# One layer of a hybrid diffusion backbone on one core: an opening with other load rows and column places, and gate and decay work spread over the level products

## The chip, the cores and the metric

The kernel runs on one core of a Trainium2 chip. TensorE (PE) multiplies, VectorE (DVE) and ScalarE (ACT) work on elements, GpSimd (POOL) does some elementwise work and issues a few DMAs, and SyncE (SP) issues the weight loads. Each engine runs its own instructions in a fixed order and waits on semaphores. The metric is the device time of one execution in microseconds (us).

## The reference

One layer over 256 latent tokens `x` and 256 context tokens `ctx`, width 2048, in fp32, with five steps:

1. `h = rms_norm(x) * g * (1 + scale) + shift`, the same for `ctx`, where scale and shift are columns of `silu(c) @ w_mod + b_mod` (`silu(c_ctx)` for the context).
2. One projection `h @ w_in` gives q, k, v of a windowed attention, `qb`, `kb`, `vb` of a gated linear attention (GLA) with 4 heads, a low-rank decay for each of its two directions, and merge gates.
3. Windowed attention (16 query heads, 4 key heads, one learned sink logit each, all context keys in the same softmax).
4. GLA in both directions; the scans of the latent tokens start from the end states of the context. In sums of log decays `b`: `o = A v` with `A[t,s] = sum_d q[t,d] k[s,d] exp(b[t,d] - b[s,d])`, plus a term `q exp(b) S`, where `S = sum_s k[s] exp(b_end - b[s]) v[s]` runs over the context.
5. Merge, output projection, gated residual, then a ConvFFN with width 5632.

The kernel keeps fp32 accuracy on PE by splitting each operand into a high and a low part (`hi`, `lo`) and adding three products: hi x hi, lo x hi, hi x lo.

## The kernel before, in words

**Weights.** `wload` loads two rows of weight tiles at a time (`raw`, 128 x 1024 numbers, 512 KB). `wsplit_raw` turns them into `whi` (ACT, L207) and `wlo` (DVE, L208). `proj_T` and `proj_nat` run the products of one weight block, all through `mm` on L83. Loads go through `load` on SP's queue (L104), and in the opening a chain of order-only dependencies keeps them in program order.

**Opening (L519 to about L640).** The two columns of the modulation (scale and shift) are needed before the first product. They are made in groups of 2, 2, 4, 4 and 4 tiles of 128 channels. `mod_both` (L305 on) makes one group of one of the two: it loads `w_mod` in tiles `mraw` of 1 MB, multiplies them with the two conditioning vectors (`pm`, L95), transposes the result on DVE (`mtr`, L324), turns it into columns with one small product (`pcol`, L95), and copies and adds on DVE (L334, L337). For each group there are so the steps `a0`, `a1` (scale: two `mraw`), `ea` (its `pcol`), and `b0`, `b1`, `eb` for shift. `affine_scale` (L488, DVE) multiplies the tokens by the scale column and the norm factor, `affine_shift` (L495 on ACT, L496 on DVE) adds the shift and splits into `h..hi` and `h..lo`. `h0` is the latent tokens, `h1` the context; their second digit is the half of the channels. `idle(n)` puts n small transposes of a constant on PE (tile `warm`, L519). The work of group 1 and 2 is put between the products of the group ahead of it: `mid()` takes so many prepared steps as the next number of a list says.

**Queue of loads at the start.** SP issues in this order: four parts of `xT`, four `mraw` (group 0), four `raw` (blocks QB, QB+512, KB, VB for the first two tiles), four parts of `ctxT`, four `mraw` (group 1), and so on. Beside it, ACT issues the constants `pack` and `crow`, and POOL issues the broadcast of `attn_sink` to 128 partitions (tile `sink`, L894) as its first DMA.

**GLA heads (`gla_A`, L703 on).** A head's piece of work is a generator whose pieces are taken, one at a time, between the products of a value projection that runs on PE meanwhile (`aside`, called from `tick` and `midway`; 16 places in one block). `with_gla` (L859) sets the rate at which pieces are taken, 0.91 pieces for each place. The pieces of a head are: the gates (four small products `pz`, then five ACT operations each, L721 to L725, and an add on DVE and on POOL); a first product `pa` of `qb` and `kb`; eight levels, in each of which ACT and DVE make scaled `q` and `k` (L766 to L775), DVE adds over halves of segments (L777 to L780) and PE multiplies them (`pa`, L95) one level later, after which DVE copies the result under a mask into `at` (L751); and at the end the decayed keys of the context: four scans on DVE (`kf`, `kg`, L800 and L802), three exponentials on ACT, two multiplies with the keys (L808, L809) and the final products `pa<-q,kf`. Each `pa` stands at a fixed place in PE's order: where its `q`, `k` or `kf` is late, all PE work waits.

Of the kernel before, what the change touches and what calls it, by code (L numbers as in the profile page):

```python
# [8 lines left out]
F32 = mybir.dt.float32  # L9
F32R = mybir.dt.float32r  # L10
U8 = mybir.dt.uint8
AF = mybir.ActivationFunctionType
# [4 lines left out]
P = 128  # L17
# [14 lines left out]
def layer_kernel(ctx, tc, A, out):  # L32
# [90 lines left out]
    def load_tokens(s):  # L123
        for i in range(4):
            k = slice((i % 2) * 4, (i % 2) * 4 + 4)
            load(xr[2 * s + i // 2][:, k, :], A["ctxT" if s else "xT"][i // 2, :, k, :])
# [22 lines left out]
    def defer(n, fn):  # L149

        later.append([n, fn])
# [37 lines left out]
    def wload(src):  # L189
        n = src.shape[0] // P  # L190
        raw = wr.tile([P, 2, 512], F32, name="raw", tag="raw")
        load(raw[:, 0:n, :], src.rearrange("(c p) d -> p c d", p=P))
        return raw
# [113 lines left out]
    def mod_both(part, t0, n, dst, put=None):  # L307
# [5 lines left out]
        def step(k0):  # L313
            if k0 == 0:
                a.append(bank(f"pm{part}_{t0}", (P, w), side=True))
            raw = M("mraw", [P, nk, w])
            load(raw, A["w_mod01"][part, t0 + k0 // nk].rearrange("p (c d) -> p c d", c=nk))
            for k in range(nk):
                kt = k0 + k
                q = 32 * (kt % 4)  # L320
                mm_b(a[0][q:q + 32, :], cS[:, kt, :], raw[:, k, :], start=(kt < 4), stop=(kt >= 12))
            if k0 == KT - nk:
                tr = W2("fb", "mtr", [P, n, 4, 32])
                V.transpose(tr.rearrange("p a b c -> p (a b c)"), a[0])  # L324
                a.append(tr)
                if put is not None:
                    put(end)
# [68 lines left out]
    def rms_scale(ss, n, shape):  # L396
# [16 lines left out]
            for (t0, n), put in zip(groups, [None, None] + 3 * [lambda fn: defer(0, fn)])]  # L413
# [5 lines left out]
    def square_sums(s):  # L419
# [3 lines left out]
        for i in range(4):  # L423
            x_ = xr[2 * s + i // 2][:, (i % 2) * 4:(i % 2) * 4 + 4, :]
            q = wr.tile([P, 4, T], F32, name="sq", tag="raw")
            if s + i:
                S.activation(q, x_, AF.Square)
            else:
                V.tensor_tensor(q, x_, x_, op=ALU.mult)
                parts.extend(q[:, k, :] for k in range(4))  # L430
                continue
# [98 lines left out]
    a0()  # L530
    a1()
# [3 lines left out]
    affine_scale(0, *groups[0])  # L535
    b1()
    raws = [wload(w_in[0:2 * P, c:c + 512]) for c in (QB, QB + 512)]
# [7 lines left out]
    raws = [wload(w_in[0:2 * P, c:c + 512]) for c in (KB, VB)]  # L545
# [4 lines left out]
    proj_T(w_in, QB, kts, [h_all(0)], add_to(lambda i: qb0[i], True))  # L550
    proj_T(w_in, QB + 512, kts, [h_all(0)], add_to(lambda i: qb0[2 + i], True))
# [14 lines left out]
    ea()  # L566
    b0()
    b1()
    for s in range(2):
        affine_scale(s, *groups[1])  # L570
# [4 lines left out]
             lambda i, b: S.activation(vb0[:, 2 + i, :], b, AF.Copy))  # L575
    early.extend(wload(w_in[2 * P:4 * P, c:c + 512]) for c in (QB, QB + 512, KB, VB))
# [19 lines left out]
    for gi, (t0, n) in enumerate(groups):  # L596
# [8 lines left out]
        if gi + 1 < len(groups):  # L605
# [3 lines left out]
            if gi == 1:  # L609
                bg_rate[:] = [0.0, 0.0]  # L610
                steps = iter([1, 2, 1, 2, 2, 0])

                def mid():
                    pin[0] = last[0]
                    for _ in range(next(steps)):
                        bg_steps.pop(0)()
                    pin[0] = None
        if t0 == 8:
            more_h(1)
        for s in range(2):  # L620
            if gi > 1:
                affine_scale(s, t0, n)
                affine_shift(s, t0, n)
# [30 lines left out]
    in_order(last_lo[0], V.tensor_scalar(nbg, nbg, -1.0, None, op0=ALU.mult).ins)  # L654
    lmask = cst.tile([P, 7, P], U8, name="lmask")
# [49 lines left out]
    def gla_A(h, kb, qb, res):  # L705
# [7 lines left out]
        for d in range(2):  # L713
            g_ = W2("fc", "gc", [P, 2, T])
            for dt in range(2):
# [11 lines left out]
                G.tensor_tensor(g_[:, dt, :], mn[:, T:2 * T], e[:, T:2 * T], op=ALU.add)  # L727
            gc.append(g_)
            yield
# [27 lines left out]
        for lv in range(8):  # L757
# [22 lines left out]
            V.tensor_tensor(sbL, sbL, sbR[:, :, 0:1].to_broadcast([P, n, m]), op=ALU.add)  # L780
            if lv == 1:
                yield
            if lv:
                products(lv - 1, *prev)
            prev = q2, k2
            yield
# [8 lines left out]
        kf = W2("fa", "kf", [P, 2, T])  # L795
        kg = W2("fa", "kg", [P, 2, T])
        tot = sm.tile([P, 2], F32, name="tot", tag="tot", bufs=2)
        one = ones[:, 0:1].to_broadcast([P, T])
        for dt in range(2):
            V.tensor_tensor_scan(kf[:, dt, :], one, gc[0][:, dt, :], 0.0, op0=ALU.mult, op1=ALU.add)  # L800
            V.memset(kg[:, dt, 0:1], 0.0)
            V.tensor_tensor_scan(kg[:, dt, 1:T], ones[:, 0:1].to_broadcast([P, T - 1]), gc[1][:, dt, 0:T - 1], 0.0,  # L802
                                 op0=ALU.mult, op1=ALU.add)
        V.tensor_scalar(tot, kf[:, :, T - 1], -1.0 / 16, None, op0=ALU.mult)
        for dt in range(2):
            S.activation(kf[:, dt, :], kf[:, dt, :], AF.Exp, scale=1.0 / 16, bias=tot[:, dt:dt + 1])
        S.activation(kg, kg, AF.Exp, scale=-1.0 / 16)
        V.tensor_tensor(kf, kf, kc, op=ALU.mult)  # L808
        V.tensor_tensor(kg, kg, kc, op=ALU.mult)  # L809
# [47 lines left out]
    def with_gla(h, kb, block):  # L857
        res = []
        beside[:] = [gla_A(h, kb, qbt, res), 0.91, 0.0]  # L859
# [33 lines left out]
    sink = cst.tile([P, 16], F32, name="sink")  # L893
    G.dma_start(sink, A["attn_sink"][0].partition_broadcast(P))  # L894
# [423 lines left out]
```

## Time and profile before

| | |
|---|---|
| median of 3 runs | 1982.68 us (1981.75 to 1982.88) |
| profiled execution | 1981.3 us, span 1979.5 us, mean granted clock 0.999 |
| PE busy in the span | 1955.1 us (99%) |
| DVE, ACT, POOL busy | 1399.8, 972.1, 44.2 us |
| DMA | 420.88 MB, mean 213 GB/s over the span |

The span runs from the first instruction to the last of the profiled execution; the execution's own time is 1.8 us longer. A line of the waits says which engine and line waited, for which producer, the sum, the count and the longest. A line of a timeline gives start, duration, engine, line, operation, output and inputs, the count, and in brackets how long the engine had been idle before and what released it; `x16` of `pm` are 8 matrix products, each of which PE records twice. A line of the table of windows gives busy time and counts for each engine in a stretch, then the granted clock of PE (1.00 is full speed), the busy share of the DMA engines and the bytes moved.

### The profile page before, as it was taken

What the parts mean: (1) busy time and instruction counts of PE and PEld (TensorE: products, weight loads), DVE (VectorE), ACT (ScalarE), POOL (GpSimd) and SP (SyncE); (2) the same over time, 40 slices, a digit from 0 to 9 for tenths busy, and PEclk for the clock granted to TensorE, in tenths of its full rate; (3) what the DMA queues carried; (4) which work ended last, traced back from release to release, by engine and by line L of the source; (5) the groups of instructions that cost most, each with busy time, mean ns of one, the idle gap of its engine ahead of it and who ended that gap; (6) DMA issues with size and microseconds to landing.
All of it is one profiled execution on the core that took longest, in us unless ns stands there. A gap on an engine that the chain in (4) does not pass through costs nothing.

```text
span 1979.5 us, 27075 instructions
## 1 busy us (share of the span) xinstructions
PE 1955.1 (99%) x10292; PEld 1636.0 (83%) x10292; DVE 1399.8 (71%) x2150; ACT 972.1 (49%) x1415; POOL 44.2 (2%) x60
## 2 busy tenths in 40 slices
PE   7999999999999999999999999999999999999999
PEld 5679988888887778888888888888888888888887
DVE  5756767876767988777766467989886555677754
ACT  4323555552345666444444445755555334555533
POOL 0010010012000000000000000000000000000000
PEclk9999999999999999999999999999999999999999
DMA  9966222336754456888888677688886566666563
GB/s 379 413 258 185 75 85 78 93 108 205 233 160 118 127 181 213 268 290 292 289 286 265 235 236 262 198 271 285 257 274 228 193 197 188 187 190 189 188 216 109
DMA packets 183666, 420.88 MB, mean 213 GB/s; under 512 B 12544, under 2 KB 12768, under 8 KB 178800
## 3 DMA queue, kind: packets, MB, share of 16 engines
q1 hardware_dynamic: 182000, 413.45, 63.9%
q0 software_dynamic: 1360, 5.54, 1.0%
q8 instruction: 80, 1.31, 0.3%
q14 instruction: 50, 0.41, 0.1%
q10 hardware_dynamic: 176, 0.17, 0.0%
HBM read 416.98 MB, written 2.13 MB: 212 GB/s over the span
## 4 chain that ended last, share of the span: by engine, by line
PE 68%; DVE 0%; ACT 0%; issue 0%; DVEq 0%
PE acc L83 52%; PE accs L83 12%; PE poa L95 1%; PE pS L95 1%; PE ptp L98 1%; PE pto L98 0%; PE ptx L98 0%; DVE wlo L208 0%; ACT s L986 0%; PE ptq L98 0%; DVE s L991 0%; DVE yd L1238 0%; DVE yd L1232 0%; DVE raw L365 0%; ACT whi L207 0%
## 5 line engine op out<-in xcount | busy, mean ns | idle before, releaser
L208 DVE TENSOR_TENSOR wlo<-raw,whi 128x1024 fp32r<-128x1024 f32 x568 | 694.1, 1223 | 439.9 <-ACT whi L207 396.4
L207 ACT ACTIVATE whi<-raw 128x1024 fp32r<-128x1024 f32 x568 | 601.5, 1060 | 765.9 <-PE acc L83 608.9
L83 PE MATMUL accs<-h,whi 128*128 128x512 f32 x704 | 176.3, 392 | 0.0
L83 PE MATMUL acc<-h,whi 128*128 128x512 f32 x640 | 160.4, 392 | 0.0
L83 PEld LDWEIGHTS accs<-h,whi 128*128 128x128 f32 x704 | 126.6, 189 | 22.7
L83 PE MATMUL acc<-whi,h01hi 128*128 128x512 f32 x352 | 139.9, 398 | 0.0
L83 PE MATMUL acc<-whi,h00hi 128*128 128x512 f32 x352 | 138.9, 395 | 0.0
L83 PE MATMUL acc<-whi,h00lo 128*128 128x512 f32 x352 | 138.1, 392 | 0.0
L83 PE MATMUL acc<-whi,h01lo 128*128 128x512 f32 x352 | 137.8, 392 | 0.0
L83 PE MATMUL acc<-whi,ah 128*128 128x512 f32 x352 | 137.0, 389 | 0.0
L83 PE MATMUL acc<-whi,al 128*128 128x512 f32 x352 | 137.0, 389 | 0.0
L83 PEld LDWEIGHTS acc<-h,whi 128*128 128x128 f32 x640 | 115.0, 189 | 20.6
L83 PEld LDWEIGHTS accs<-h,wlo 128*128 128x128 f32 x704 | 96.0, 190 | 6.9
L83 PE MATMUL acc<-wlo,h01hi 128*128 128x512 f32 x352 | 98.7, 396 | 0.0
L83 PE MATMUL accs<-h,wlo 128*128 128x256 f32 x704 | 98.2, 282 | 0.0
L83 PE MATMUL acc<-wlo,h00hi 128*128 128x512 f32 x352 | 97.8, 394 | 0.0
L83 PE MATMUL acc<-wlo,ah 128*128 128x512 f32 x352 | 94.3, 389 | 0.0
L83 PEld LDWEIGHTS acc<-h,wlo 128*128 128x128 f32 x640 | 87.4, 190 | 6.3
L83 PE MATMUL acc<-h,wlo 128*128 128x256 f32 x640 | 89.4, 282 | 0.0
L365 DVE CUSTOM_DVE_ANT_0 raw<-raw,csrow,pack 128x1024 f32<-128x1024 f32 x64 | 81.4, 1281 | 0.0
L83 PEld LDWEIGHTS acc<-whi,ah 128*128 128x128 f32 x352 | 66.1, 188 | 13.7
L83 PEld LDWEIGHTS acc<-whi,al 128*128 128x128 f32 x352 | 66.1, 188 | 13.7
(377 smaller groups left out, 3558.1 us busy)
## 6 DMA issues: line engine op xcount, KB each, us to landing
raw<-in_w_in SPq DMA_DIRECT2D x208, 512.0 KB, 4.2
raw<-in_w_up SPq DMA_DIRECT2D x176, 512.0 KB, 4.1
raw<-in_w_modT SPq DMA_DIRECT2D x128, 512.0 KB, 4.4
raw<-in_w_down SPq DMA_DIRECT2D x88, 512.0 KB, 3.6
mraw<-in_w_mod SPq DMA_DIRECT2D x32, 1024.0 KB, 12.1
raw<-in_w_attn_o SPq DMA_DIRECT2D x32, 512.0 KB, 5.0
raw<-in_w_gla_o SPq DMA_DIRECT2D x32, 512.0 KB, 5.1
raw<-in_w_out SPq DMA_DIRECT2D x32, 512.0 KB, 4.7
```

Source lines behind the costliest of these rows:

```text
L83: r = pe_seq(PE.matmul(*a, **k))
L95: return pe_seq(after(PE.matmul(*a, **k)))
L98: return pe_seq(after(PE.transpose(*a)))
L207: j = S.activation(hi[:, 0:n, :], raw[:, 0:n, :], AF.Copy).ins
L208: i = V.tensor_tensor(lo[:, 0:n, :], raw[:, 0:n, :], hi[:, 0:n, :].bitcast(F32), op=ALU.subtract).ins
L365: i0 = V.tensor_tensor_reduce(out=raws[i], in0=raws[i], in1=row[0], scale=1.0, scalar=d if h else bmod[:, b0:b0 + 1], op0=ALU.mult, op1=AL ...
```

## The change

**Opening loads.** `xT` and `ctxT` come as two loads of 1 MB, with one row of 8 KB for each partition in place of two loads with rows of 4 KB. The first four weight tiles come from a new input `w_first`, packed on the host, with one row of 4 KB for each partition in place of two of 2 KB. The last load of the shift column of groups 0 and 1 is split into two halves of 512 KB. The broadcast of `sink` moves from the first place of POOL's queue to the place behind `cw`, ahead of `lm` and eight gate weights (`wtm`).

SP's order from the first load on (`xr_85` to `xr_88` are the tokens, `mraw` the modulation weights, `raw` the weight tiles):

```order
-L104 DMA xr_85<-in_xT 128x1024 x2
-L104 DMA xr_86<-in_xT 128x1024 x2
-L104 DMA mraw<-in_w_mod 128x2048 x4
-L104 DMA raw<-in_w_in 128x2x512 x4
-L104 DMA xr_87<-in_ctxT 128x1024 x2
-L104 DMA xr_88<-in_ctxT 128x1024 x2
-L104 DMA mraw<-in_w_mod 128x2048 x4
+L1353 UNCONDITIONAL_BRANCH
+L104 DMA xr_85<-in_xT 128x2048
+L104 DMA xr_86<-in_xT 128x2048
+L104 DMA mraw<-in_w_mod 128x2048 x3
+L104 DMA mraw<-in_w_mod 128x1024 x2
+L104 DMA raw<-in_w_first 128x1024 x4
+L104 DMA xr_87<-in_ctxT 128x2048
+L104 DMA xr_88<-in_ctxT 128x2048
+L104 DMA mraw<-in_w_mod 128x2048 x3
+L104 DMA mraw<-in_w_mod 128x1024 x2
```

Each token tile now has one row in place of two, and behind three `mraw` stand two halves.

**Opening order.** Six transposes (`idle(6)`) are added between `a0` and `a1`, and six before `b1`. The first eviction of `qb0` is an ACT copy as before; its instructions are now remembered, and the squares of the context tokens on ACT are tied behind them. In group 1, `b0` and `b1` come ahead of `ea`, so that all products `pm` of the group come ahead of its first `pcol`. In group 2, the scale's `pcol` moves to a later place together with the multiplication of the tokens (`affine_scale`), and all 16 products of the shift column are taken in one place.

PE at the end of the KB block of group 1 (`pm_4_673`, after it `pm_4_693`, is the shift of group 2, `pcol_4_724`/`pcol_4_740` its columns, `pcol_4_676` the scale's columns; `acc<-h..,wlo` are the last 16 products of KB, `acc<-whi,h00hi` the first of VB). Before, behind the last products of KB:

```order
L83 MATMUL acc<-h00hi,wlo 128x256
L83 MATMUL acc<-h10hi,wlo 128x256
L83 MATMUL acc<-h00hi,wlo 128x256
L83 MATMUL acc<-h10hi,wlo 128x256
L95 MATMUL pm_4_673<-mraw,cS 32x512 x8
L95 MATMUL pcol_4_724<-mtr,pack 32x32
L83 MATMUL acc<-whi,h00hi 128x512
```

After, ahead of the last 16 products of KB:

```order
L83 MATMUL acc<-h10lo,whi 128x256
L95 MATMUL pcol_4_676<-mtr,pack 32x32
L95 MATMUL pm_4_693<-mraw,cS 32x512 x16
L83 MATMUL acc<-h00hi,wlo 128x256
L83 MATMUL acc<-h10hi,wlo 128x256
```

Before, 8 of the shift's 16 products stood ahead of KB's last 16 and 8 behind; now all 16 stand ahead of them, with the scale's columns directly before.

**GLA.** Each of the four gate pieces is now a piece of its own (two before), the extra stop at level 1 is gone, and the rate goes from 0.91 to 0.97, which takes 15 pieces over the 16 places in place of 14. The four scans move from the end of the head into levels 2 and 3, `tot` and the exponentials into level 4, the two multiplies with the keys into level 6; each is tied behind the last add of its level. `kf` and `kg` use another pool (`fb` in place of `fa`).

DVE in the third head (`kf<-ones,gc` and `kg<-ones,gc` are the scans; `segs` the adds of a level; `q`, `k` the scaled operands). Before, at the end of the head:

```order
L794 TENSOR_TENSOR q_3652<-q_3652,qb 128x512
L794 TENSOR_TENSOR q_3653<-q_3653,qb 128x512
L62 TENSOR_TENSOR ats<-at,ats 128x256
L800 SCALAR_TENSOR_TENSOR kf<-ones,gc 128x256
L801 MEMSET kg 128x1
L802 SCALAR_TENSOR_TENSOR kg<-ones,gc 128x255
L62 TENSOR_TENSOR ats<-pa,ats 128x256
L800 SCALAR_TENSOR_TENSOR kf<-ones,gc 128x256
L801 MEMSET kg 128x1
L802 SCALAR_TENSOR_TENSOR kg<-ones,gc 128x255
```

After, between two levels:

```order
L835 TENSOR_TENSOR segs<-segs 128x64x4
L806 COPY_PREDICATED at<-lmask,pa 128x256
L767 SCALAR_TENSOR_TENSOR kf<-ones,gc 128x256
L768 MEMSET kg 128x1
L212 TENSOR_TENSOR wlo<-raw,whi 128x1024
L769 SCALAR_TENSOR_TENSOR kg<-ones,gc 128x255
L823 TENSOR_TENSOR q_3487<-q_3487,qb 128x512
L830 TENSOR_TENSOR k_3491<-k_3491,kb_2020 128x512
L832 TENSOR_TENSOR segs<-segs 128x32x8
L833 TENSOR_TENSOR segs<-segs 128x32x8
L834 TENSOR_TENSOR segs<-segs 128x32x8
L835 TENSOR_TENSOR segs<-segs 128x32x8
```

The scans stood behind the last level; now a pair of them stands between the adds of level 2 and the next `q` and `k`, and the other pair one level later.

The diff, cut to what the text speaks of:

```diff
     def load_tokens(s):
-        for i in range(4):
-            k = slice((i % 2) * 4, (i % 2) * 4 + 4)
-            load(xr[2 * s + i // 2][:, k, :], A["ctxT" if s else "xT"][i // 2, :, k, :])
+        for i in range(2):
+            load(xr[2 * s + i], A["ctxT" if s else "xT"][i])
...
+    def first_w(i):
+        raw = wr.tile([P, 2, 512], F32, name="raw", tag="raw")
+        load(raw.rearrange("p k d -> p (k d)"), A["w_first"][i])
...
-            load(raw, A["w_mod01"][part, t0 + k0 // nk].rearrange("p (c d) -> p c d", c=nk))
+            src = A["w_mod01"][part, t0 + k0 // nk].rearrange("p (c d) -> p c d", c=nk)
+            if t0 < 4 and part == 0 and k0:
+                load(raw[:, 0:nk // 2, :], src[:, 0:nk // 2, :])
+                load(raw[:, nk // 2:nk, :], src[:, nk // 2:nk, :])
+            else:
+                load(raw, src)
...
-                S.activation(q, x_, AF.Square)
+                j = S.activation(q, x_, AF.Square).ins
+                if s and i in (0, 2):
+                    in_order(evicted[i + 1], j)
...
     a0()
+    idle(6)
     a1()
     idle(4)
...
-    raws = [wload(w_in[0:2 * P, c:c + 512]) for c in (KB, VB)]
+    raws = [first_w(i) for i in range(2, 4)]
     load_tokens(1)
     i, j = affine_shift(0, *groups[0])
     hold.append(i)
     hold_hi.extend([None, j])
-    proj_T(w_in, QB, kts, [h_all(0)], add_to(lambda i: qb0[i], True))
-    proj_T(w_in, QB + 512, kts, [h_all(0)], add_to(lambda i: qb0[2 + i], True))
+    evicted = []
+    for j in range(2):
+        proj_T(w_in, QB + j * 512, kts, [h_all(0)],
+               lambda i, b, j=j: evicted.append(S.activation(qb0[2 * j + i], b, AF.Copy).ins))
...
-    ea()
     b0()
     b1()
-    for s in range(2):
-        affine_scale(s, *groups[1])
+    ea()
+    affine_scale(0, *groups[1])
...
+    affine_scale(1, *groups[1])
...
-                steps = iter([1, 2, 1, 2, 2, 0])
+                steps = iter([1, 2, 1, 4, 0, 0])
+
+                def next_columns():
+                    if pend:
+                        pend.pop(0)()
+
+                def scale_2():
+                    next_columns()
+                    for s in range(2):
+                        affine_scale(s, *groups[2])
+
+                also = iter([next_columns] * 3 + [scale_2, next_columns, lambda: affine_shift(0, *groups[2])])
 
                 def mid():
                     pin[0] = last[0]
+                    next(also)()
...
-            if gi > 1:
+            if gi > 2:
                 affine_scale(s, t0, n)
+            if gi > 2 or (gi == 2 and s):
...
+    sink = cst.tile([P, 16], F32, name="sink")
+    G.dma_start(sink, A["attn_sink"][0].partition_broadcast(P))
...
+                yield
             gc.append(g_)
-            yield
...
+        def decays(dt, level):
+            one = ones[:, 0:1].to_broadcast([P, T])
+            i = V.tensor_tensor_scan(kf[:, dt, :], one, gc[0][:, dt, :], 0.0, op0=ALU.mult, op1=ALU.add).ins
+            V.memset(kg[:, dt, 0:1], 0.0)
+            j = V.tensor_tensor_scan(kg[:, dt, 1:T], ones[:, 0:1].to_broadcast([P, T - 1]), gc[1][:, dt, 0:T - 1],
+                                     0.0, op0=ALU.mult, op1=ALU.add).ins
+            in_order(level, i, j)
+
+        def decayed(level):
+            tot = sm.tile([P, 2], F32, name="tot", tag="tot", bufs=2)
+            in_order(level, V.tensor_scalar(tot, kf[:, :, T - 1], -1.0 / 16, None, op0=ALU.mult).ins)
+            for dt in range(2):
+                S.activation(kf[:, dt, :], kf[:, dt, :], AF.Exp, scale=1.0 / 16, bias=tot[:, dt:dt + 1])
+            S.activation(kg, kg, AF.Exp, scale=-1.0 / 16)
+
+        def decayed_keys(level):
+            in_order(level, V.tensor_tensor(kf, kf, kc, op=ALU.mult).ins)
+            in_order(level, V.tensor_tensor(kg, kg, kc, op=ALU.mult).ins)
+
+        beside_levels = {2: lambda i: decays(0, i), 3: lambda i: decays(1, i), 4: decayed, 6: decayed_keys}
...
-            V.tensor_tensor(sbL, sbL, sbR[:, :, 0:1].to_broadcast([P, n, m]), op=ALU.add)
-            if lv == 1:
-                yield
+            level = V.tensor_tensor(sbL, sbL, sbR[:, :, 0:1].to_broadcast([P, n, m]), op=ALU.add).ins
             if lv:
                 products(lv - 1, *prev)
             prev = q2, k2
+            if lv in beside_levels:
+                beside_levels[lv](level)
...
-        for dt in range(2):
-            V.tensor_tensor_scan(kf[:, dt, :], one, gc[0][:, dt, :], 0.0, op0=ALU.mult, op1=ALU.add)
-            V.memset(kg[:, dt, 0:1], 0.0)
-            V.tensor_tensor_scan(kg[:, dt, 1:T], ones[:, 0:1].to_broadcast([P, T - 1]), gc[1][:, dt, 0:T - 1], 0.0,
-                                 op0=ALU.mult, op1=ALU.add)
-        V.tensor_scalar(tot, kf[:, :, T - 1], -1.0 / 16, None, op0=ALU.mult)
-        for dt in range(2):
-            S.activation(kf[:, dt, :], kf[:, dt, :], AF.Exp, scale=1.0 / 16, bias=tot[:, dt:dt + 1])
-        S.activation(kg, kg, AF.Exp, scale=-1.0 / 16)
-        V.tensor_tensor(kf, kf, kc, op=ALU.mult)
-        V.tensor_tensor(kg, kg, kc, op=ALU.mult)
...
-        beside[:] = [gla_A(h, kb, qbt, res), 0.91, 0.0]
+        beside[:] = [gla_A(h, kb, qbt, res), 0.97, 0.0]
```

## What the change does to the time: the prediction

> **What bounds the kernel now.** I read the page first, then the waits of PE in the two stretches that the change touches, then the windows and timelines there.
>
> ```profile
> span 1979.5 us, 27075 instructions
> PE 1955.1 (99%) x10292; PEld 1636.0 (83%) x10292; DVE 1399.8 (71%) x2150; ACT 972.1 (49%) x1415; POOL 44.2 (2%) x60
> ```
>
> PE is busy in 99% of the span. No PE work goes away: 12 small transposes are added. So the change can win only waits of PE, and the slow clock. They are few. The waits of PE from 0 to 80 us, and from 200 to 460 us (the four GLA heads):
>
> ```profile
> PE pm L95 <- DMA mraw<-in_w_mod: 3.0, 3, 1.4
> PE pcol L95 <- DVE mtr L324: 2.6, 4, 0.8
> ...
> PE acc L83 <- ACT qb L503: 0.4, 1, 0.4
> ...
> PE pa L95 <- DVE q L768: 3.1, 4, 1.1
> PE pa L95 <- DVE kf L808: 2.5, 3, 1.0
> ```
>
> With 0.4 and 0.7 for `h00hi` and `h10hi` (rows of the opening below) that is 7.1 us in the opening, and 5.6 us in the heads: the whole stake is about 13 us of 1981.3. The windows show what stands behind the opening's waits (busy time of the engines, granted clock, share and GB/s of DMA last):
>
> ```profile
> 5.00:7.00 2.00, 1.96 (x9) 1.96 (x10) 1.30 (x2) 1.90 (x4) 0.00 (x0) 1.00 1.04 158
> 7.00:10.20 3.20, 3.20 (x12) 2.69 (x11) 0.73 (x2) 3.11 (x3) 0.51 (x1) 1.00 1.02 397
> 10.30:20.20 9.90, 6.86 (x66) 3.41 (x64) 5.67 (x17) 1.89 (x3) 0.00 (x0) 1.00 1.00 421
> 20.30:26.70 6.40, 5.85 (x40) 3.67 (x41) 2.99 (x9) 3.36 (x5) 0.00 (x0) 0.75 1.05 396
> 26.80:31.80 5.00, 4.72 (x40) 4.52 (x38) 4.17 (x6) 3.88 (x6) 0.00 (x0) 1.00 1.04 421
> 60.00:112.00 52.00, 50.08 (x381) 37.15 (x380) 35.00 (x73) 11.56 (x16) 0.00 (x0) 1.00 1.01 402
> ```
>
> The DMA engines are full in all these stretches, so a load's landing is set by what was streamed ahead of it, and time saved in the stream stays saved through the opening. From 5 to 7 us they are as full and move only 158 GB/s: that is where `sink` (128 pieces of 64 bytes, landed at 7.9) is in the stream.
>
> **The loads.** `sink` out of the start: 2 us at 158 in place of 397 GB/s are 0.48 MB missing, or 1.2 us. The 2 KB rows of the four `raw` ran at 396 GB/s (20.3 to 26.7), 8 KB rows of `mraw` at 421 (10.3 to 20.2): 2.1 MB in 5.0 in place of 5.3 us, 0.3 us. The tokens' rows grow from 4 KB to 8 KB; the window of `ctxT` (26.8 to 31.8) has 421 already, so nothing. The split of two `mraw` costs nothing in the stream by the same row, and its two more issues on SP (0.33 us each) wait nowhere, since loads are issued 9 to 15 us before they land (rows below). Gain of the stream: 1.5 us; at worst `sink` only moves its price to other packets and 0.3 remain.
>
> [...]
>
> At its new place `sink` is 1.2 us ahead of `lm` and the gate weights. The waits of PE from 76 to 224 us hold nothing but
>
> ```profile
> PE acc L83 <- DVE wlo L208: 0.5, 2, 0.3
> ```
>
> and no DMA, so I cost that at nothing; without cover it is 1.2 us.
>
> **The opening, step by step.** PE in the timeline (at the end the issue of the last `mraw` of group 1 and of group 2, each with its time to landing):
>
> ```profile
> 16.28 0.66 PE L519 MATMUL warm<-pack 128*128 128x128 f32 x4
> 16.92 0.24 PE L95 MATMUL pcol<-mtr,pack 128*32 128x16 f32 x2
> 17.78 1.07 PE L95 MATMUL pm<-mraw,cS 128*32 128x256 f32 x16 [0.62 <-DMA mraw<-in_w_mod]
> 20.27 1.93 PE L95 MATMUL pm<-mraw,cS 128*32 128x256 f32 x16 [1.43 <-DMA mraw<-in_w_mod]
> 24.96 0.39 PE L83 MATMUL acc<-h00hi,whi 128*128 128x256 f32 x1 [0.42 <-ACT h00hi L495]
> ...
> 41.46 0.20 PE L95 MATMUL pcol<-mtr,pack 128*32 128x16 f32 x1 [0.57 <-DVE mtr L324]
> 44.15 0.38 PE L83 MATMUL acc<-h10hi,whi 128*128 128x256 f32 x1 [0.71 <-ACT h10hi L495]
> 47.32 0.23 PE L95 MATMUL pcol<-mtr,pack 128*32 128x16 f32 x2 [0.32 <-DVE mtr L324]
> 62.26 0.25 PE L95 MATMUL pcol<-mtr,pack 128*32 128x32 f32 x2 [0.84 <-DVE mtr L324]
> 66.45 1.92 PE L95 MATMUL pm<-mraw,cS 128*32 128x512 f32 x16
> 70.40 1.92 PE L95 MATMUL pm<-mraw,cS 128*32 128x512 f32 x16
> 73.16 0.25 PE L95 MATMUL pcol<-mtr,pack 128*32 128x32 f32 x2 [0.84 <-DVE mtr L324]
> ...
> L104 SPq DMA_DIRECT2D mraw<-in_w_mod x1: 328/328/328, 26.8 to 26.8; - x1
> DMA to landing us min/median/max: 15.0/15.0/15.0
> ...
> L104 SPq DMA_DIRECT2D mraw<-in_w_mod x1: 328/328/328, 58.5 to 58.5; - x1
> DMA to landing us min/median/max: 9.4/9.4/9.4
> ```
>
> - *Turns.* Four transposes take 0.66 us, so six take 1.0. The six before `b1` start when `b0` ends, about 18.1 (its load lands at 16.3, but PE comes there at 17.15), and end at 19.1, when the split load has landed (20.2 less 1.5). Their cover is what is left of the old wait, so they cost 0.4. They keep PE busy in a stretch (16.7 to 20.1) behind which the clock fell:
>
> ```profile
> 13.29:16.69 3.40, 2.39 (x36) 1.16 (x36) 1.97 (x5) 0.83 (x2) 0.00 (x0) 1.00 1.01 426
> 16.70:20.11 3.41, 1.53 (x21) 0.55 (x18) 2.02 (x10) 0.00 (x0) 0.00 (x0) 1.00 0.98 407
> 20.12:23.53 3.41, 3.26 (x23) 1.62 (x24) 0.47 (x2) 1.06 (x1) 0.00 (x0) 0.50 1.05 390
> ```
>
>   After 2.39 us of work in 3.4 the next stretch had clock 1.00, after 1.53 it had 0.50. Now about 3 us of work stand there, so I take 1.00. Then `b1` runs from 19.1 to 20.2 and the first main product comes, with the old distances, at 22.5 in place of 24.96: 2.4 us won. If the clock falls all the same, the first products run at half speed to 23.5: 0.5 lost.
> - *Eviction of `qb0`.* Tying the squares behind it frees 0.4.
> - *Group 1.* `pcol` no longer stands between the products `pm`: 0.57 goes. But PE now comes to the last `pm` of the group at 39.0 (42.4 less 2.4, 0.4, 0.6), and its load lands at 40.3 (26.8 + 15.0 less 1.5). The load is late next: what was won ahead of it, beyond what the stream won, is lost again, and so is a lost clock. Behind it come half its products and the column; `h10hi` is late by about the same, and the first product is at 41.2 in place of 44.15: 3.0. The wait at 47.32 goes: 3.3.
> - *Group 2.* With the scale's `pcol` later its 0.84 goes: 4.1. PE comes to the shift's products at 62.3, and all 16 stand there, behind them everything on PE. The fourth load lands at 66.4 (58.5 + 9.4 less 1.5), PE is there at 65.2: a new wait of 1.2. Then half of 1.92, the last 16 products of KB (70.40 - 66.45 - 1.92 = 2.0), whose time now covers `mtr`, and `pcol`: VB begins at 69.6 in place of 73.3. DVE has KB's evictions, the scale multiplications and `mtr` in these 5 us; they fit with about 0.7 to spare.
>
> So the opening gives 3.7. It hangs on one landing: with nothing won in the stream it is 2.2, with no wait there 4.9. Behind it no PE wait is on a load, so it stays.
>
> **The GLA heads.** The head's own rows: PE of the second head (its first and fifth product `pa`), the final products of the third, DVE ahead of one product, and the moved operations.
>
> ```profile
> 289.52 1.16 PE L95 MATMUL pa<-q,kb 128*128 128x128 f32 x8 [1.07 <-DVE q L768]
> 304.06 1.13 PE L95 MATMUL pa<-q,k 128*128 128x128 f32 x8
> 388.60 1.10 PE L95 MATMUL pa<-q,kf 128*128 128x256 f32 x4 [0.99 <-DVE kf L808]
> ...
> 303.23 0.68 DVE L775 TENSOR_TENSOR k<-k,kb 128x512 f32<-128x512 f32 x1
> ...
> L802 DVE TENSOR_TENSOR_SCAN kg<-ones,gc 128x255 f32<-128x255 f32 x8 | 5.5, 683 | 0.0
> L808 DVE TENSOR_TENSOR kf<-kf,kb 128x512 f32<-128x512 f32 x4 | 2.8, 688 | 0.4 <-ACT kf L806 0.4
> ...
> 289.50:317.50 28.00, 27.98 (x148) 23.24 (x149) 26.54 (x55) 13.57 (x33) 0.00 (x0) 1.00 0.36 108
> ```
>
> Removed: the final wait, since `kf` is ready long before (2.5 over the heads), and the first wait, since the gates come piece by piece and the first product stands 4 main products, 0.9 us, later (3.1). Added to the levels: four scans, 2.7, and two multiplies, 1.4: 4.1 us in each head, in a phase in which DVE is busy 26.54 of 28.0 us, with 1.4 idle. And it had little in hand: `k` ended at 303.91, 0.15 us ahead of its product, the fifth. The scans come between, 1.4 and again 1.4 us. In the order after, the fifth product stands 0.4 us later against the first than before; so it waits between 0.7 (all of DVE's idle time used) and 2.2 (none); I take 1.4, the middle, because only part of that idle time lies ahead of it. What PE waits there the later products have as room, so nothing is added for the multiplies. For the third head the same; in the fourth, where the order has more main products ahead of that place, an estimate of 0.5; in the first, whose products stand widest apart, 0.3. Together 3.6 of new waits against 5.6 removed: 2.0 won. The ends: 2.2 in each head, 8.8 against 5.6, a loss of 3.2; or no new wait, a gain of 5.6.
>
> **Sum.** 3.7 + 2.0 = 5.7, so the profiled execution goes from 1981.3 to 1975.6. The median is 1.4 above that execution: 1977.0.
>
> **The rivals.**
> - *The heads win nothing.* The new waits equal the removed ones. For it: 1.4 in all four heads is 5.6. Against it: the first and fourth have more room. Then 3.7: 1979.0.
> - *The levels hide the moved work.* For it: DVE's 71% over the span; against it: 95% here. Then 3.7 + 5.6: 1973.4.
> - *The stream wins nothing.* The bytes of `sink` are few, and other packets could have been slowed by the start, not by it. Against it: nothing else in the first 32 us runs below 396. Opening 2.2, in all 4.2: 1978.5.
> - *Slower: DVE becomes the bound of the levels.* All 4.1 us stretch each phase, 16.4 in four heads, less 5.6 removed and 3.7: 7.1 more, 1989.8. It decides from new waits of 3.3 us a head on, (5.6 + 3.7 + 4.0) / 4. Against it: the scans were on DVE ahead of the same final products before, so a head as a whole has no more work on DVE.
>
> **How the numbers follow.** Forecast 0.42, the heads win nothing 0.19, all hidden 0.17, stream wins nothing 0.10, slower 0.12. About 0.2%, 4 us, is what a measurement can tell from no change. The forecast, the hidden levels and half of the stream's case lie beyond 4 us faster: 0.64. The rest of the stream's case (4.2 is near the bound) and the heads' case lie within: 0.24. Slower by 4: 0.12. The range runs from 1972.5 (hidden levels and a slightly better opening) to 1982.7 (heads lose 3.2, opening 3.7, and a little).
>
> **What the profile after would show.** Right: the wait on `mraw` in the opening falls to about 2.5 us with one new wait near 65 us on the last `mraw` of group 2; the clock is 1.00 in all windows from 16 to 27 us; VB begins near 69.6; the waits on `kf` are gone, and `pa <- q` or `k` has some 3.5 us in the middle levels. Wrong: `pa` waits of over 9 us in the heads, DVE idle no more in the levels, or 5 to 7 us still at 158 GB/s.

## The result

| | before | after |
|---|---|---|
| median (5 runs each, same chip) | 1982.68 us (1981.26 to 1983.28) | 1973.95 us (1973.76 to 1974.24) |
| ratio | | 0.9959 (95% interval 0.9947 to 0.9972) |
| profiled execution, span | 1981.3, 1979.5 us | 1973.76, 1971.9 us |

The change makes the kernel 8.7 us faster by the medians and 7.5 us by the profiled executions; 5.7 were forecast (1977.0, range 1972.5 to 1982.7). The executions of the kernel before fall in two groups, near 1981.5 and near 1982.9; three of these five lie in the upper group and the profiled one in the lower, and beside the experiments the median before was 1981.67, 1981.56 and 1981.47, so 7.5 is the better figure for the change.

The page of the changed kernel, its waits of PE from 0 to 80 us, and those of the four heads (196 to 470 us):

```profile
span 1971.9 us, 27072 instructions
PE 1952.4 (99%) x10304; PEld 1636.1 (83%) x10304; DVE 1397.9 (71%) x2150; ACT 971.2 (49%) x1415; POOL 41.2 (2%) x60
...
PE warm L534 <- DMA pack<-in_k_pack: 6.8, 1, 6.8
PE pm L95 <- DMA mraw<-in_w_mod: 1.6, 2, 1.2
PE acc L83 <- ACT h10hi L507: 0.5, 1, 0.5
PE acc L83 <- ACT h00hi L507: 0.5, 1, 0.5
PE pr L460 <- DVE sq L451: 0.4, 1, 0.4
PE pr L460 <- DVE sq L445: 0.2, 1, 0.2
...
PE pa L95 <- DVE k L830: 3.5, 5, 1.0
```

All waits on `mtr` and on `kf` are gone, and all on `q`. The waits on `k` in the levels are new, and so is the wait on a load near 66 us. PE's timeline at the places that the prediction named:

```profile
23.40 0.39 PE L83 MATMUL acc<-h00hi,whi 128*128 128x256 f32 x1 [0.46 <-ACT h00hi L507]
40.31 0.64 PE L95 MATMUL pm<-mraw,cS 128*32 128x256 f32 x8 [0.35 <-DMA mraw<-in_w_mod]
41.52 0.38 PE L83 MATMUL acc<-h10hi,whi 128*128 128x256 f32 x1 [0.54 <-ACT h10hi L507]
66.31 1.07 PE L95 MATMUL pm<-mraw,cS 128*32 128x512 f32 x8 [1.24 <-DMA mraw<-in_w_mod]
69.59 0.50 PE L83 MATMUL acc<-whi,h00hi 128*128 128x512 f32 x1
```

VB of group 1 begins at 69.59 in place of 73.34. To see where the rest of the gain lies, I set the start of the same instruction in both traces side by side. The rows on which the readings rest are, in the kernel before (the first three) and in the changed one:

```profile
73.34 0.50 PE L83 MATMUL acc<-whi,h00hi 128*128 128x512 f32 x1
209.56 0.63 PE L95 MATMUL pz<-wgl 128*128 128x512 f32 x2
463.93 0.39 PE L95 MATMUL po<-v3h,ats 128*128 128x512 f32 x1
...
205.79 0.40 PE L95 MATMUL pz<-wgl 128*128 128x512 f32 x1
456.75 0.39 PE L95 MATMUL po<-v3h,ats 128*128 128x512 f32 x1
```

All places:

```
                                       before    after   difference
first product of VB, group 1             73.34    69.59     -3.75
first h01hi product                     125.50   121.73     -3.77
first gate product of head 1            209.56   205.79     -3.77
first output product of head 1          266.70   262.14     -4.56
  of head 2                             329.97   323.96     -6.01
  of head 3                             393.73   386.99     -6.74
  of head 4                             463.93   456.75     -7.18
attention, first value split            549.04   541.86     -7.18
```

So the opening gives 3.8, the heads 3.4, and nothing else moves until the last few microseconds. The experiments below are read in the same way, at the place 209.56 (opening) and between it and 463.93 (heads). Each experiment ran beside the kernel before, not beside the changed kernel; so a few tenths of a microsecond against 1973.95 tell nothing.

### The profile page after: what moved, and what is told of

Same layout as the page of the kernel before. It is cut to its first block, busy times and chain, and to the rows that moved or that the text cites. A ratio compares the mean times of both kernels' runs of the same rounds, so it can differ in the third digit from the quotient of the medians.

```text
span 1971.9 us, 27072 instructions
## 1 busy us (share of the span) xinstructions
PE 1952.4 (99%) x10304; PEld 1636.1 (83%) x10304; DVE 1397.9 (71%) x2150; ACT 971.2 (49%) x1415; POOL 41.2 (2%) x60
## 4 chain that ended last, share of the span: by engine, by line
PE 95%; DVE 3%; DMA 1%; ACT 1%; issue 0%; DVEq 0%; ACTq 0%
PE acc L83 73%; PE accs L83 12%; PE pa L95 2%; PE poa L95 1%; PE pm L95 1%; PE pS L95 1%; PE po L95 1%; PE ptp L98 1%; DVE wlo L212 1%; DMA mraw<-in_w_mod 1%; PE pto L98 0%; DMA pack<-in_k_pack 0%; DVE q L823 0%; DVE k L830 0%; PE ptq L98 0%
```

## The experiments

**e1: the opening alone.** The changed kernel with the heads of the kernel before (`gla_A` as before and rate 0.91).

> All of the change but the GLA heads, which are as before. Theory A (the two stages add up: opening 3.8, heads 3.4 by the place of the same work in the two traces): the first product of VB of group 1 near 69.6 us, the heads wait 5.6 us as before, time about 1977.4 (1973.95 + 3.4 to 3.6), 4 to 5 us under the kernel before. Theory B (the 1.2 us by which the medians differ more than the two profiled executions belong to the heads): about 1979, 3.7 under.

Measured: 1977.52 us (1977.35 to 1979.77, 10 runs), before 1981.67. The heads wait as in the kernel before:

```profile
PE pa L95 <- DVE q L799: 3.2, 4, 1.1
PE pa L95 <- DVE kf L839: 2.5, 3, 1.0
```

The median is as theory A had it, and theory B is out: the heads carry about 3.6 us. Two of the ten runs took 1979.7, and the profiled one is among these. Its windows show why:

```profile
64.00:67.40 3.40, 1.52 (x16) 0.31 (x16) 2.79 (x8) 0.00 (x0) 0.00 (x0) 1.00 1.00 412
67.41:70.82 3.41, 3.41 (x18) 2.18 (x11) 1.47 (x3) 0.00 (x0) 0.00 (x0) 0.50 1.04 414
```

PE waits twice for loads there (0.46 and 1.42 us), works 1.52 of 3.40 us, and runs at half the clock for the 3.41 us behind it; opening and all are then 1.5 us earlier than before in place of 3.8. The kernel before had the same thing at 20.12 to 23.53, after 1.53 us of work. Both stretches of half clock are 3.41 us long, and they start at different places (20.12 in the kernel before, 67.41 here). PE was not idle throughout in the 3.4 us ahead of either: it worked 1.53 us there before and 1.52 here.

**e2: the heads alone.** The kernel before with `gla_A` and the rate 0.97 of the changed one.

> The kernel before with only the change in the GLA heads. Theory A: VB at 73.3 us as before, waits of PE on q, k or kf in the heads 3.5 us in place of 5.6, but the place of the work after the heads 3.4 us earlier; time about 1979.2, 3.4 under the kernel before. My prediction had 2.0 for it: 1980.7. If the spread of the kernel before (1981.3 to 1983.3) comes from its opening, it stays: about 2 us between the runs.

Measured: 1978.16 us (1977.64 to 1979.78, 10 runs), before 1981.67: 3.5 us. At the place 209.56 it is 0.3 later than before, at 463.93 it is 2.7 earlier, so 3.0 in the heads. Here the waits are

```profile
PE pa L95 <- DVE k L799: 3.8, 5, 1.1
```

The two stages add up within 0.4 us. This execution had no stretch of half clock in the windows where the kernel before has it (1.00 in all from 13.29 to 26.90 us), and yet its first product of the context stands at 44.45, not ahead of the 44.15 of the kernel before: what a full clock won at 24 us (the first main product at 23.97 in place of 24.96), a longer wait for `qb` lost at 32 us (1.67 in place of 0.41). The slow clock at 20 us was free in the kernel before. The ten runs still span 2.1 us, so that spread does not come from the heads of the kernel before.

**e3: no turns.**

```diff
     a0()
-    idle(6)
     a1()
...
-    idle(6)
     b1()
```

> The changed kernel without the two groups of six transposes. Theory A (turns only keep the clock, and the landing of the load at 66.3 us hides what a slow clock costs): a window at clock 0.50 in the first 27 us again, first product of VB still near 69.6, median within 0.5 us of 1974.0. Theory C (turns carry the gain of the opening): about 1 to 2.5 us slower, 1975 to 1976.5. If the turns do not hold the clock, no window differs in clock from the changed kernel.

Measured: 1974.41 us (1974.26 to 1975.99, 5 runs). In the median the turns are worth 0.5 us at most. The expected stretch of half clock below 27 us did not come: the clock from 13.29 to 26.90 us is 1.00 without the turns too. It came at 66.7 us in the profiled execution (1975.99), behind the wait for the last load of group 2 and a stretch with 1.53 us of work, and its opening is 1.8 us ahead of the kernel before in place of 3.8:

```profile
63.32:66.73 3.41, 1.53 (x17) 0.18 (x12) 3.12 (x8) 0.00 (x0) 0.00 (x0) 1.00 0.99 410
66.74:70.15 3.41, 3.41 (x15) 1.75 (x16) 1.04 (x2) 0.00 (x0) 0.00 (x0) 0.50 1.05 420
```

The first main product was at 22.16, earlier than with the turns (23.40); the loads from 38 to 40 us took most of that back (waits of 0.50, 0.22 and 0.64 in place of one of 0.35; the first product of the context is at 41.09 in place of 41.52). So the turns do not carry the gain, and whether they keep the clock is not shown by one run in five.

**e4: `sink` first again.** Its DMA moves from behind `cw` to the start of POOL's queue.

> The changed kernel with the broadcast of sink back at the first place of POOL's queue. Theory A (the stream is full, and the opening ends at one landing): the last shift load of group 2 lands 1.2 us later, VB near 70.8, time about 1975.2. Rival (the slot of sink is not lost to the stream, or pack lands earlier again and pays it back): no change, 1974.0 within 0.3.

Measured: 1975.57 us (1975.12 to 1975.75, 6 runs). The opening is 2.3 us ahead of before in place of 3.8, and the last shift load is later by as much:

```profile
67.75 1.06 PE L95 MATMUL pm<-mraw,cS 128*32 128x512 f32 x8 [1.25 <-DMA mraw<-in_w_mod]
```

67.75 against 66.31: 1.44 us. In this run `pack` lands later too (8.2 in place of 6.8), and all of PE's work ahead of the load with it; but PE's wait for the load stays as it was (1.25), so the load itself is later. The bytes moved up to 66 us say the same, first of the changed kernel, then of this one:

```profile
0.00:66.00 66.00, 56.09 (x455) 40.92 (x455) 40.05 (x93) 28.67 (x43) 0.82 (x5) 1.00 0.99 399
0.00:66.00 66.00, 56.17 (x455) 41.75 (x455) 38.64 (x90) 28.66 (x43) 1.38 (x6) 1.00 0.99 390
```

9 GB/s over 66 us are 0.6 MB, or 1.4 us at the 414 GB/s that the stream runs at from 25 to 60 us, in the kernel before and in the changed one alike. In this run the broadcast of 8 KB in 64-byte pieces cost the full stream 1.4 us, and the opening ended at that landing.

**e5: the decays untied.** The scans are written behind the last level again, without ties to a level, but `kf` and `kg` stay allocated early, in the pool `fb`.

```diff
-            if lv in beside_levels:
-                beside_levels[lv](level)
...
+        for dt in range(2):
+            V.tensor_tensor_scan(kf[:, dt, :], one, gc[0][:, dt, :], 0.0, op0=ALU.mult, op1=ALU.add)
```

> The changed kernel with the scans, exponentials and multiplies of the decays back at the end of each head; gate pieces and rate stay. Theory A (the moved decays trade the final waits against waits in the levels, and the gain of the heads comes from the gate pieces): final waits on kf of 2 to 3 us come back, the 3.5 us of waits in the levels go, time 1973.0 to 1974.5, as the changed kernel within 1 us. Rival (the moved decays carry the gain): 2 to 3 us slower, 1976 to 1977.

Measured: 1979.39 us (1978.63 to 1980.91, 10 runs). Neither theory had this. The waits of the heads:

```profile
PE pa L95 <- DVE q L802: 6.7, 4, 1.8
PE pa L95 <- DVE k L809: 1.5, 1, 1.5
```

DVE shows that the kernel is not what its label says:

```profile
285.71 0.69 DVE L830 TENSOR_TENSOR_SCAN kf<-ones,gc 128x256 f32<-128x256 f32 x1
286.33 1.19 DVE L832 TENSOR_TENSOR_SCAN kg<-ones,gc 128x255 f32<-128x255 f32 x1
...
287.76 0.68 DVE L830 TENSOR_TENSOR_SCAN kf<-ones,gc 128x256 f32<-128x256 f32 x1
...
288.68 0.68 DVE L832 TENSOR_TENSOR_SCAN kg<-ones,gc 128x255 f32<-128x255 f32 x1
...
289.60 0.68 DVE L802 TENSOR_TENSOR q<-q,qb 128x512 f32<-128x512 f32 x1
```

With the buffers free and no tie, the scheduler put all four scans right behind the gates, ahead of the first `q`, and the first product waits 1.5 to 1.8 us in each head. The same work costs some 5 us more at that place (the profiled execution is the longest of the ten: it also runs at half the clock from 224.2 to 227.6, behind the first of these waits); the question of the rival stays open here and is put again in e9.

**e6: gates as before.** Two gate pieces, the extra stop at level 1, rate 0.91; the decays stay in the levels.

> The changed kernel with two gate pieces, the extra stop at level 1 and the rate 0.91 as before; the decays stay in the levels. Theory A: the first waits on q (3.1 us, with the restarts 3.7) come back on top of about 3.5 in the levels, time 1976.5 to 1978. Rival (first waits belong to the levels' load on DVE, not to the gate pieces): within 1 us of 1974.

Measured: 1978.62 us (1978.01 to 1978.96, 10 runs); the heads are 4.6 us longer than in the changed kernel and 1.1 longer than before.

```profile
PE pa L95 <- DVE k L830: 3.5, 8, 0.9
PE pa L95 <- DVE q L823: 2.5, 4, 1.1
```

The first waits are back (2.5 of 3.1) and the waits of the levels are still there: theory A, though the time is 0.6 above its range. Moving the decays without the gates makes the heads 1.1 us slower.

**e7: columns as before.** The order of groups 1 and 2 in the opening as in the kernel before; loads and turns stay.

> The changed kernel with the places of the columns in groups 1 and 2 as before; loads and turns stay. Theory A (the opening ends at one landing, the columns' waits lie ahead of it): waits on mtr of 0.6, 0.8 and 0.8 us come back, the wait for the last load near 66 us goes; first product of VB 0.3 to 1 us later than 69.6, time 1974.3 to 1975. Rival (the columns carry most of the opening's gain): 2 us slower or more.

Measured: 1975.35 us (1975.18 to 1975.47, 6 runs).

```profile
PE pcol L95 <- DVE mtr L333: 2.6, 4, 0.8
```

The old waits are back to the digit, the wait for the load is gone, and the opening is 1.7 us later than in the changed kernel. That lies between the two theories: the moved columns carry 1.7 of the 3.8, more than the 0.3 to 1 that I expected of them. The loads, the turns and the eviction without the columns' places still win 2.1; PE then has no wait on a load left, so how much of that is the stream's is not shown by this run.

**e8: the last load later.** The last four products of group 2's shift go behind the last 16 products of KB, their column into the middle of VB.

```diff
-                steps = iter([1, 2, 1, 4, 0, 0])
+                steps = iter([1, 2, 1, 3, 1, 0])
```

> The changed kernel with the four products of the last shift load of group 2 taken one place later, behind the last 16 products of KB. Theory A (the new wait of 1.24 us on that load is the end of the opening): the wait goes, first product of VB near 68.3, time about 1972.7, and no run 1.5 to 2 us above the others, since the clock no longer falls behind that wait. Rival (another wait takes its place: the shift's column on mtr, 0.7 to 0.8 us): 1973.5.

Measured: 1973.90 us (1973.58 to 1974.07, 4 runs), no change. The wait of 1.24 is gone and VB begins at 68.6, 1.0 earlier. Then the time is lost again: the column's product, now inside VB, takes 0.4 (VB's first eviction is 0.6 earlier), and the next block, for whose tokens the column is now late, waits 0.19 on `h00hi` and starts 0.3 ahead; its first four products, each close behind the `h00hi` or `h00lo` that it needs, take 0.5 longer than in the changed kernel. At 125.50 the kernel is 0.2 behind the changed one. The rival was right, with another wait than it named.

**e9: the decays last.** As e5, but with `kf` and `kg` in the pool `fa`, allocated behind the last level as in the kernel before, so that their buffers come free only there.

> The changed kernel with the decays where they were before: in the pool fa and behind the last level, so that nothing lets them start early; gate pieces and rate stay. Theory A (the two parts of the heads each remove their own waits): no wait on q for the first products, final waits on kf of 2 to 3 us, no waits in the levels; heads within 1 us of the changed kernel, 1973.5 to 1975. Theory D (the parts need each other, since the gate pieces leave less room at the end of a head): 2 us slower or more, with final waits above 4 us.

Measured: 1972.88 us (1972.75 to 1973.40, 4 runs).

```profile
PE pa L95 <- DVE kf L837: 2.8, 3, 1.1
PE pa L95 <- DVE k L806: 0.4, 1, 0.4
```

No wait on `q`, no waits in the levels but one, the final waits back: theory A, and the heads are 1.0 us shorter than in the changed kernel. So the gate pieces alone win 4.4 us, and moving the decays loses 1.0 of it. e6 says the same from the other side (1.1 longer than before with the decays alone).

**e10 and e11: other levels for the decays.**

```diff
-        beside_levels = {2: lambda i: decays(0, i), 3: lambda i: decays(1, i), 4: decayed, 6: decayed_keys}
+        beside_levels = {1: lambda i: decays_f(0, i), 2: lambda i: decays_f(1, i), 3: lambda i: decays_g(0, i), 4: lambda i: decays_g(1, i), 5: decayed, 6: decayed_keys}
```

in e10, where `decays_f` and `decays_g` are the halves of `decays`, and in e11 `{4: decays(0), 5: decays(1), 6: decayed, 7: decayed_keys}`.

> The changed kernel with one scan in each of the levels 1 to 4 in place of two in levels 2 and 3, tot and the exponentials in level 5. If the waits in the levels come from two scans in a row (1.4 us) ahead of a k that had 0.15 us in hand: waits of the second and third head fall from 1.0 to 0.3 to 0.7 us each, 0.5 to 1 us faster, 1973.2. If only the sum of the work ahead of the fifth product counts: no change, 1974.

> The changed kernel with the scans in levels 4 and 5, tot and the exponentials in level 6, the multiplies in level 7. By the traces the last two products have 0.9 and 1.5 us in hand: the fifth product then no longer waits, a later one waits 0.5 us or less, waits in the heads 1 to 2 us in place of 3.5, time 1972 to 1973. Rival (the decays end too late): final waits on kf of 1 to 3 us, 1974 or slower.

Measured: e10 1972.91 us (1972.35 to 1973.11, 4 runs), e11 1974.00 us (1973.37 to 1974.41, 5 runs). In e10 the fifth product of the second and third head waits 0.5 in place of 1.0, as expected for two scans in a row; in the fourth head two waits (1.07 and 0.88) stand where there were three of together 1.5. Its heads are 1.1 us shorter:

```profile
300.29 1.13 PE L95 MATMUL pa<-q,k 128*128 128x128 f32 x8 [0.49 <-DVE k L833]
362.89 1.13 PE L95 MATMUL pa<-q,k 128*128 128x128 f32 x8 [0.50 <-DVE k L833]
```

In e11 the wait moved to a later product and is as long:

```profile
308.77 1.13 PE L95 MATMUL pa<-q,k 128*128 128x128 f32 x8 [1.22 <-DVE k L830]
372.45 1.13 PE L95 MATMUL pa<-q,k 128*128 128x128 f32 x8 [0.74 <-DVE k L830]
```

Now the seventh product waits, for a `k` with the second pair of scans directly ahead of it. What it had in hand in the kernel before (0.9) was no longer there: in the order of e11 it stands 72 main products behind the first product, before it was 76, which is 0.9 us earlier; less the 1.4 of the scans that leaves the 1.2 that it waits, nearly. e9 and e10 are about 1 us under the changed kernel and 8.6 under the kernel before beside them; they are the fastest that I ran.

**e12: rows as before.** Tokens in four loads with 4 KB rows, the first weight tiles with 2 KB rows.

> The changed kernel with the rows of the tokens and of the first four weight tiles as before (4 KB and 2 KB, four and four loads). By the rates of the windows (396 and 421 GB/s) the last shift load of group 2 lands 0.3 us later and the time is 0.3 us more, 1974.3; if the tokens' rows cost too, 0.6. [...]

Measured: 1975.64 us (1974.57 to 1976.62, 6 runs), three near 1974.6 and three near 1976.5.

```profile
PE warm L530 <- DMA pack<-in_k_pack: 5.0, 1, 5.0
PE pm L95 <- DMA mraw<-in_w_mod: 4.0, 6, 1.4
```

The last load's products start at 66.88 in place of 66.31, 0.6 later. But in e9, e10 and e11, whose loads are those of the changed kernel, they start at 66.45, 66.87 and 66.95. So the price of the rows cannot be read from the landing: 0.3, 0.6 and nothing are all within what it varies. The bytes moved do show one. From 20 to 30 us, where the first weight tiles are in the stream, the three kernels with 2 KB rows (before, e2, e12) run at 402 to 405 GB/s and the ten with 4 KB rows and a late `sink` at 421 to 424. The changed kernel and e12:

```profile
20.00:30.00 10.00, 9.41 (x81) 8.00 (x81) 7.77 (x15) 7.64 (x10) 0.00 (x0) 1.00 1.02 422
20.00:30.00 10.00, 9.41 (x75) 8.62 (x74) 7.66 (x14) 8.20 (x11) 0.00 (x0) 1.00 1.05 405
```

That is 0.17 MB, or 0.4 us of the stream. (The 4 KB rows are also packed side by side in `w_first`, so length and place in memory are not told apart.) Up to 66 us e12 runs at 395 GB/s, the ten at 398 or 399: 0.2 to 0.3 MB less. How much of this the time gains stays open. What differs besides is the number of waits on loads (six; none to four in the runs with the new rows and the turns) and `pack`, which lands 1.7 us earlier. Whether the three runs near 1976.5 have a slow clock behind those waits, as in e1, is not shown: the mean granted clock of each is 0.999, that of the three near 1974.6 is 1.000, 0.999 and 1.000, and the profiled one is among the latter.

## Why the prediction was right

The time lay in the range, on the forecast side, and the gain of the profiled executions (7.5) was 1.8 above the forecast (5.7). By its own steps:

- **The opening, 3.7: right, 3.8.** The mechanism held: the last load as the end of the opening, a new wait of 1.2 (1.24), VB at 69.6 (69.59), the first product of the context at 41.2 (41.52), nothing lost behind it. That it came to a tenth is partly luck: in e5, e6 and e9 to e11, which have the same opening, VB begins between 69.56 and 70.26. The stream won about what was forecast for it (1.5): up to 66 us it had moved 0.6 MB more than before (399 in place of 390 GB/s), which is 1.4 us. e4 gives 1.4 back by `sink` alone (I took 1.2); e12 gives about 0.5 back by the rows. The two overlap, so their prices do not add up: with the old rows, the kernel before (390) and e12 (395), which differ in the order of work too, are 0.8 us apart. Against the rival in which the stream wins nothing I said that nothing else in the first 32 us runs below 396 GB/s; that left out the first 4 us (18 and 289, and 61 and 254 in the changed kernel), and it is e4 that answers the rival. e7 adds that without the moved columns 1.7 of the 3.8 stays in the old waits; the columns with the old stream, and the tie behind the eviction of `qb0` (0.4), were not tried alone. e8 limits the step: with the wait for the last load gone the opening is no shorter, since the columns behind it are then late.
- **Longer rows, 0.3: in the stream 0.4, in the time not settled** (e12). The windows show a price of the 2 KB rows of the weight tiles (405 against 422 GB/s from 20 to 30 us). The stretch with the 64-byte pieces of `sink` ran at 158 GB/s in the kernel before (5 to 7 us), the same stretch without them at 432 in the changed one.
- **Turns and the clock: the step was wrong and did not count.** I let the six transposes cost 0.4 and put the first product at 22.5; it came at 23.40. The whole start is later, since `pack` lands at 6.8 in place of 5.0 behind the longer token rows, and the squares of the tokens with it. I had given `pack` no thought; with the old rows (e12) it lands at 5.0, and the first product is at 22.09. PE then comes to the loads after they have landed, so the turns had no wait to hide in: without them (e3, `pack` 0.3 earlier) the first product is at 22.16, so they cost about 1.0. The waits on loads fell to 1.6 and not only to 2.5. The wait at 40 us hid the late start (0.35 left of an expected 1.3), as the prediction said it would hide a lost clock. e3 shows that without turns the clock at 20 us stays full (1.00), and e2 that the slow clock there (0.50) had cost the kernel before nothing (the first product of the context at 44.45 without it, at 44.15 with it).
- **The heads, 2.0: too small, 3.4.** The sum of the waits was right: 3.5 are left in the levels, 3.6 were forecast, and 5.6 went. They lie where I put them in the second and third head (1.0 each on the fifth product, 1.4 forecast), not in the fourth (1.5 on three products, 0.5 forecast) or the first (none, 0.3 forecast). The term that was mis-sized is the price of a wait. In starts of instructions, each wait of PE in the heads makes a gap 0.16 us longer than the wait that is listed (1.07 listed, 1.23 in starts), and there are five where there were seven: 0.3. The other 1.0 us is in many gaps of under 0.2 us, between small and large products above all. It belongs to the change of the gates: counted in this way (gain of the heads less the waits removed, less 0.16 for each), nothing is left over in e1 and e6, which have the gates of the kernel before, and 0.7 to 1.5 in the profiled executions of all others but e5, whose first head ran partly at half the clock. Which part of that change makes it (the pieces, the stop at level 1, the rate) was not tried.
- **Which part wins: not seen.** The prediction priced the two parts of the heads as one balance, removed against new. e6 and e9 separate them: gate pieces 4.4 won, moved decays 1.0 lost. The sum of the waits came out right all the same, so it could not show this. The rival in which the levels of DVE become the bound was half true: from the second head's first product on DVE is busy 27.77 of 28.0 us (26.54 before), the "DVE idle no more" that I had named as a sign of being wrong. It costs a microsecond, since the final waits that it was to remove (2.5) are fewer than the waits it makes (3.5).
- **The median.** I put it 1.4 above the profiled execution for both kernels. After, it is 0.2 above, and beside the experiments the median of the kernel before lay 0.2 to 0.4 above it. One execution's time against a median of three was too thin a base for a shift of 1.4 us.

## What to carry to other kernels

Where a stage ends at one landing in a full stream, ask first what the stream carries ahead of it that nobody needs yet: here a broadcast of 8 KB in 64-byte pieces cost as much as 0.6 MB of weights. The work moved off the end of a chain into an engine that was 95% busy (26.54 of 28.0 us) traded 2.5 us of waits for 3.5; taking it apart by experiment (one part alone, the other alone) showed that the moved decays would be better left out of this change. A wait's price was not only what the table of waits lists (1.07 listed, 1.23 in starts): count starts of the same instruction in both traces.

## What the runs showed of the hardware that I had not expected

- Four times (the kernel before, e1, e3, e5) a stretch of 3.4 us with 1.52 to 1.58 us of PE work was followed by half the clock for 3.4 us; after 1.42 us (the kernel before, 3.05 to 6.46), 1.88 us (e2, 16.70 to 20.11), 2.22 us (the changed kernel, 62.85 to 66.27) and 2.39 us (the kernel before, 13.29 to 16.69) it stayed full (1.00). The same waits do not always do it: 0.46 and 1.42 us for loads gave the slow clock in e1, 0.47 and 1.42 us at the same place in e12 did not. What decides it is not shown. Two runs of ten in e1 took 2.2 us longer; one of them is the profiled one, which has the slow clock.
- A small load of one queue landed later beside longer rows of another: `pack` (161 KB, ScalarE's queue) landed at 5.0 to 5.3 us beside token rows of 4 KB, whether `sink` was ahead of it (the kernel before, e2) or not (e12), at 6.5 to 6.9 beside rows of 8 KB, and at 8.2 with `sink` ahead of it as well (e4). The number of token loads (four or two) changed with the rows, so the two are not told apart.
- Of the scheduler rather than the chip: without a tie, a buffer that comes free early let it move work to a costly place (e5); the pool of the tiles, and their allocation behind the last level, had kept the scans at the end (e9).
